# Residual loads and stores of two image pairs at a time in a 3x3 convolution with residual add

## Chip, cores, metric

One core of a Trainium2 chip. The metric is the device time in microseconds (us) of one execution; lower is better. Beside the timed figure, every run lists the span of its core, which is the time from the program's first to its last instruction; the difference between the two is called "the part outside the span" below.

## The reference

A 3x3 convolution, padding 1, plus a residual, all float32: x and residual are 16 x 64 x 64 x 64 (16.8 MB each), the weight is 64 x 64 x 3 x 3, the output is 16.8 MB.

```python
for b in range(batch):
    for co in range(c_out):
        for ci in range(c_in):
            for kh in range(k):
                for kw in range(k):
                    output[b, co] += weight[co, ci, kh, kw] * x_pad[b, ci, kh:kh+h, kw:kw+w]
return (output + residual).astype(np.float32)
```

## The kernel before

Two images make a pair: 128 partitions (image and channel) of 4096 pixels, 2 MB. SyncE issues all large transfers but one (ScalarE loads half of the first x). ScalarE (ACT) casts x into bf16 with even and odd rows in different partitions, TensorE (PE) does 24 matmuls per image into one of two PSUM halves, VectorE (DVE) adds PSUM and residual in place in `ro`, and `ro` is stored. All 16 MB of residual stay in SBUF. Everything but the last stores stands in one critical section, with hand-written semaphores. At its end SyncE waits for all engines, then the last two stores are issued, and a second critical section on GpSimd waits for the earlier ones.

```python
    ro = [pool.tile([128, NPIX], FP32, name=f"ro{p}") for p in range(NPAIR)]   # 8 tiles of 2 MB
    # ...
    with tc.tile_critical(no_gpsimd_drain=True):
        for p in range(NPAIR):
            if p >= NXR:                                     # NXR = 3 buffers of x
                nc.sync.wait_ge(s_half, 2 * (p - NXR) + 3)
            # ... (the weight is loaded after the first half of x)
                load_x(p)
            load_ro(p)                                       # a semaphore of its own
        for p in range(NEARLY):                              # NEARLY = 6
            nc.sync.wait_ge(s_add, 2 * p + 3)
            store(p).then_inc(s_out, 16)
        # ... (identity, zeros, casts of x and of the weight)
        for n in range(B):
            p, im = divmod(n, 2)
            # ...
            if im == 0:
                nc.vector.wait_ge(s_r[p], 16)
            # ... two adds per image
        # ... (TensorE)
    for p in range(NEARLY, NPAIR):                           # two stores of 2 MB
        store(p)
    with tc.tile_critical(sync_engine=mybir.EngineType.Pool, no_gpsimd_drain=True):
        nc.gpsimd.wait_ge(s_out, 16 * NEARLY)
```

## Time and profile before

| | before |
|---|---|
| time, median of 3 | 122.9 us (122.8 to 123.06) |
| span of the profiled run | 121.2 us |
| bytes moved | 33.70 MB read, 16.78 MB written |
| DMA rate, slices 4 to 38 | 427 or 433 GB/s in all but three |
| PE ends / DVE ends / last store lands | 99.5 / 104.1 / 120.2 us |

How to read it: the DMA engines are full from about 3 us to 119 us, so the time is bytes over rate plus a start and an end. The lines that carry this are in the prediction.

### The profile page before, as it was taken

To read this page: it belongs to the slowest core of one execution; us is meant where nothing else is said; L and a number is where in the kernel's file an instruction comes from. 1 tells how busy PE (TensorE), PEld (TensorE's weight loads), DVE (VectorE), ACT (ScalarE), POOL (GpSimd) and SP (SyncE) were. 2 spreads that over 40 slices of the span, in tenths; PEclk is the share of its full clock that TensorE was granted. 3 is DMA by queue.
4 is the path that set the end of the run, shared out by engine and by line. 5 is a ranking of instruction groups with operands and counts; after the bars stand their busy time and mean duration, and the time that the engine had idled before them with its cause. 6 is when DMAs were issued, how large, how long until landed. Compare 5 with 4: busy or idle time off the path is not lost.

```text
span 121.2 us, 736 instructions
## 1 busy us (share of the span) xinstructions
PE 87.7 (72%) x389; PEld 10.7 (9%) x105; DVE 76.0 (63%) x40; ACT 63.1 (52%) x37; POOL 2.4 (2%) x16
## 2 busy tenths in 40 slices
PE   0033499999999999999999999999999980000000
PEld 0021001101010101010101010101010100000000
DVE  0005300889898898989889898898989889300000
ACT  4049969938966984993993994896000000000000
POOL 5200000000000000000000000000000000000000
PEclk9999999999999999999999999999999999755555
DMA  6999999999999999999999999999999999999993
GB/s 168 427 444 433 433 433 433 433 427 433 433 427 427 433 433 427 427 433 427 433 433 433 433 433 422 433 389 433 433 433 433 422 433 433 433 433 433 427 433 151
DMA packets 3744, 50.48 MB, mean 417 GB/s; under 512 B 416, under 2 KB 544, under 8 KB 544
## 3 DMA queue, kind: packets, MB, share of 16 engines
q1 hardware_dynamic: 3600, 49.43, 96.3%
q10 hardware_dynamic: 144, 1.05, 2.0%
HBM read 33.70 MB, written 16.78 MB: 417 GB/s over the span
## 4 chain that ended last, share of the span: by engine, by line
PE 71%; DVEq 2%; DVE 2%; issue 0%
PE ps L86 53%; PE ps L85 17%; DVEq L129 2%; DVE ro L201 2%
## 5 line engine op out<-in xcount | busy, mean ns | idle before, releaser
L201 DVE TENSOR_TENSOR ro<-ps,ro 64x2048 f32<-64x2048 f32 x32 | 73.2, 2289 | 17.7 <-PE ps L86 17.2
L86 PE MATMUL ps<-xp,wl 128*128 128x504 bf16 (+1 forms) x288 | 80.0, 388 | 0.2
L173 ACT CAST xp<-xr 64x2048 bf16<-64x2048 f32 x16 | 30.3, 1896 | 19.3 <-DMA xr<-in_x_dram 17.1
L85 PE MATMUL ps<-xp,wl 128*128 128x504 bf16 (+1 forms) x92 | 35.8, 389 | 3.4 <-PEq L222 3.4
L177 ACT CAST xp<-xr 64x2048 bf16<-64x2048 f32 x16 | 30.4, 1897 | 0.4
L85 PEld LDWEIGHTS ps<-xp,wl 128*128 128x128 bf16 x96 | 9.5, 99 | 79.1 <-issue 79.1
L189 DVE CAST wl<-ps 32x192 bf16<-32x192 f32 x8 | 2.8, 348 | 10.4 <-PE ps L214 10.3
L214 PE MATMUL ps<-ident,wraw 128*32 128x128 f32 x9 | 2.1, 412 | 8.1 <-DMA wraw<-in_weight_dram 8.1
L214 PEld LDWEIGHTS ps<-ident,wraw 128*32 128x32 f32 x9 | 1.2, 137 | 8.6 <-issue 8.1
L173 ACT ACT_TABLE_LOAD x1 | 1.3, 1283 | 1.1 <-SPq L129 1.1
L182 ACT CAST wl<-ps 32x192 bf16<-32x192 f32 x4 | 1.2, 306 | 0.0
L160 POOL MEMSET xp<- 64x64 bf16 x4 | 0.6, 147 | 0.2
L159 POOL MEMSET xp<- 64x64 bf16 x4 | 0.6, 145 | 0.2
L148 POOL TENSOR_SCALAR_AFFINE_SELECT ident<-ident 128x128 f32<-128x128 f32 x1 | 0.3, 295 | 0.2 <-POOL ident L146 0.2
L162 POOL MEMSET wl<- 64x192 bf16 x1 | 0.3, 253 | 0.1
L161 POOL MEMSET wl<- 64x192 bf16 x1 | 0.3, 252 | 0.1
L146 POOL MEMSET ident<- 128x128 f32 x1 | 0.2, 205 | 0.7 <-SPq L129 0.7
L257 POOL MEMSET const-uint8-127<- 128x1 uint8 x1 | 0.1, 113 | 0.0
L257 POOL MEMSET const-bfloat16-1.0<- 128x1 bf16 x1 | 0.1, 112 | 0.0
L257 POOL MEMSET const-float32-1.0<- 128x1 f32 x1 | 0.1, 109 | 0.0
L257 POOL MEMSET const-float32-0.0<- 128x1 f32 x1 | 0.1, 104 | 0.2 <-issue 0.2
## 6 DMA issues: line engine op xcount, KB each, us to landing
ro<-in_residual_dram SPq DMA_DIRECT2D x8, 2048.0 KB, 21.9
out_dram<-ro SPq DMA_DIRECT2D x8, 2048.0 KB, 28.2
xr<-in_x_dram SPq DMA_DIRECT2D x7, 2048.0 KB, 17.5
xr<-in_x_dram SPq DMA_DIRECT2D x1, 1024.0 KB, 7.0
xr<-in_x_dram ACTq DMA_DIRECT2D x1, 1024.0 KB, 7.6
wraw<-in_weight_dram SPq DMA_DIRECT2D x1, 144.0 KB, 6.9
```

What stands on the lines that cost most here:

```text
L85: return e.matmul(out=out_, lhsT=lhsT, rhs=rhs, start=start, stop=stop, skip_group_check=True)
L86: return e.add_instruction(mybir.InstMatmult(name=nc.get_next_instruction_name(), engine=PE, ins=[e.lower_ap(rhs), e.lower_ap(lhsT)], outs ...
L129: with tc.tile_critical(no_gpsimd_drain=True):
L159: nc.gpsimd.memset(t[0:64, 0, :], 0.0).then_inc(s_id, 1)
L160: nc.gpsimd.memset(t[64:128, J, :], 0.0).then_inc(s_id, 1)
L173: i = nc.scalar.copy(out=t[64:128, 0:J, :], in_=x4[hp, :, 0, :])
L177: nc.scalar.copy(out=t[0:64, 1 : J + 1, :], in_=x4[hp, :, 1, :]).then_inc(s_pack, 1)
L182: i = nc.scalar.copy(**weight_block(h, *b))
L189: i = nc.vector.tensor_copy(**weight_block(h, *b))
L201: i = nc.vector.tensor_tensor(out=o4[hp, :, par, :], in0=psj[64 * par : 64 * par + 64, :, :], in1=o4[hp, :, par, :], op=ADD)
L214: i = nc.tensor.transpose(out=tp[0:32, t // 3, 128 * (t % 3) : 128 * (t % 3) + 128], in_=wraw3[:, :, t], identity=ident[:, :])
L257: nc = _bacc.Bacc("TRN2", target_bir_lowering=False, num_devices=1)
```

## The change

Its intent: fewer and larger transfers (4 MB), x loaded further ahead, one store and not two behind the critical section, and 13 semaphores where there were 20. The residual of pairs 2 and 3, 4 and 5, 6 and 7 comes in one transfer each, counted on two semaphores; DVE therefore waits five times and not eight. All stores are of two pairs.

```diff
-    NEARLY = 6
+    NSTORE = NPAIR // 2
+    RES = (slice(0, 1), slice(1, 2), slice(2, 4), slice(4, 6), slice(6, 8))
@@
-    ro = [pool.tile([128, NPIX], FP32, name=f"ro{p}") for p in range(NPAIR)]
+    ro = pool.tile([128, NPAIR, NPIX], FP32)
@@
-    s_r = [sem(f"s_r{p}") for p in range(NPAIR)]
+    s_r = [sem(f"s_r{i}") for i in range(2)]
...  (s_wt is dropped, its counts go on s_id)
@@
-    def load_ro(p):
-        nc.sync.dma_start(out=ro[p][:, :], in_=res_bc[128 * p : 128 * p + 128, :]).then_inc(s_r[p], 16)
-
-    def store(p):
-        return nc.sync.dma_start(out=out_bc[128 * p : 128 * p + 128, :], in_=ro[p][:, :])
+    def load_ro(i):
+        if i >= 2:
+            nc.sync.wait_ge(s_r[i % 2], 16 * (i // 2))
+        nc.sync.dma_start(out=ro[:, RES[i], :], in_=res_bc[:, RES[i], :]).then_inc(s_r[i % 2], 16)
+
+    def store(k):
+        pairs = slice(2 * k, 2 * k + 2)
+        return nc.sync.dma_start(out=out_bc[:, pairs, :], in_=ro[:, pairs, :])
@@
-            load_ro(p)
-        for p in range(NEARLY):
-            nc.sync.wait_ge(s_add, 2 * p + 3)
-            store(p).then_inc(s_out, 16)
+            if p in (0, 1, 3, 5, 7):
+                load_ro((p + 1) // 2)
+        for k in range(NSTORE - 1):
+            nc.sync.wait_ge(s_add, 4 * k + 5)
+            store(k).then_inc(s_out, 16)
@@
-            if im == 0:
-                nc.vector.wait_ge(s_r[p], 16)
+            if im == 0 and p in first:
+                i = first.index(p)
+                nc.vector.wait_ge(s_r[i % 2], 16 * (i // 2 + 1))
@@
-    for p in range(NEARLY, NPAIR):
-        store(p)
+    store(NSTORE - 1)
     with tc.tile_critical(sync_engine=mybir.EngineType.Pool, no_gpsimd_drain=True):
-        nc.gpsimd.wait_ge(s_out, 16 * NEARLY)
+        nc.gpsimd.wait_ge(s_out, 16 * (NSTORE - 1))
```

More of the change, by code (lines that the diff above doesn't have):

```diff
@@ L37 @@
     NXP = 4
-    NEARLY = 6
-    res_bc = residual.rearrange("b c h w -> (b c) (h w)")
-    out_bc = out.rearrange("b c h w -> (b c) (h w)")
+    NZERO = 4 + 2 * NXP
+    NSTORE = NPAIR // 2
+    RES = (slice(0, 1), slice(1, 2), slice(2, 4), slice(4, 6), slice(6, 8))
+    res_bc = residual.rearrange("(p b) c h w -> (b c) p (h w)", b=2)
+    out_bc = out.rearrange("(p b) c h w -> (b c) p (h w)", b=2)
     x_bc = x.rearrange("b c h w -> (b c) (h w)")
@@ L59 @@
     s_x = [sem(f"s_x{i}") for i in range(NXR)]
-    s_r = [sem(f"s_r{p}") for p in range(NPAIR)]
+    s_r = [sem(f"s_r{i}") for i in range(2)]
     s_out = sem("s_out")
     s_id = sem("s_id")
-    s_wt = sem("s_wt")
     s_half = sem("s_half")
@@ L178 @@
             if n == 0:
-                nc.scalar.wait_ge(s_wt, 1)
+                nc.scalar.wait_ge(s_id, NZERO + 1)
                 for b in blocks[4:]:
@@ L182 @@
                         i = nc.scalar.copy(**weight_block(h, *b))
-                i.then_inc(s_wt, 1)
-        nc.vector.wait_ge(s_wt, 1)
+                i.then_inc(s_id, 1)
+        nc.vector.wait_ge(s_id, NZERO + 1)
         for k, b in enumerate(blocks[:4]):
@@ L191 @@
                     i.then_inc(s_bank, 2)
-        i.then_inc(s_wt, 1)
+        i.then_inc(s_id, 1)
+        first = [pairs.start for pairs in RES]
         for n in range(B):
@@ L195 @@
             hp = slice(64 * im, 64 * im + 64)
-            o4 = ro[p].rearrange("q (j two w) -> q j two w", two=2, w=W)
+            o4 = ro[:, p, :].rearrange("q (j two w) -> q j two w", two=2, w=W)
             psj = ps[n % 2].rearrange("q c j w -> q (c j) w")
-            if im == 0:
-                nc.vector.wait_ge(s_r[p], 16)
+            if im == 0 and p in first:
+                i = first.index(p)
+                nc.vector.wait_ge(s_r[i % 2], 16 * (i // 2 + 1))
             for par in range(2):
@@ L207 @@
                 i.then_inc(s_add if par == 0 or n == B - 1 else s_bank, 1)
-        nc.tensor.wait_ge(s_id, 4 + 2 * NXP)
+        nc.tensor.wait_ge(s_id, NZERO)
         nc.tensor.wait_ge(s_w, 16)
@@ L216 @@
             )
-        i.then_inc(s_wt, 1)
-        nc.tensor.wait_ge(s_wt, 3)
+        i.then_inc(s_id, 1)
+        nc.tensor.wait_ge(s_id, NZERO + 3)
         with nc.Fori(0, B // NXP, 1, engines=[PE]):
```

## The prediction

> **What bounds the kernel now.** I read the page's slices first, then the chain, then the DMA queue's own waits, then a table by stage, then the times at which single transfers landed.
>
> ```profile
> DVE  0005300889898898989889898898989889300000
> DMA  6999999999999999999999999999999999999993
> GB/s 168 427 444 433 433 433 433 433 427 433 433 427 427 433 433 427 427 433 427 433 433 433 433 433 422 433 389 433 433 433 433 422 433 433 433 433 433 427 433 151
> DMA packets 3744, 50.48 MB, mean 417 GB/s; under 512 B 416, under 2 KB 544, under 8 KB 544
> HBM read 33.70 MB, written 16.78 MB: 417 GB/s over the span
> PE 71%; DVEq 2%; DVE 2%; issue 0%
> ```
>
> The DMA row is full in 38 of 40 slices at one rate, whether it reads (first two thirds) or writes (last third). The chain says "PE 71%", but its last pieces end at about 104 us: PE finishes at 99.5, DVE at 104.1, and the span is 121.2. The last 17 us are stores, so the chain names an engine that is merely nearly as long, and the bound is the DMA. The stage table says the same (columns: window, length, busy time by engine, clock, DMA share, GB/s):
>
> ```profile
> 3.00:4.00 1.00, 0.00 (x0) 0.00 (x0) 0.00 (x0) 0.00 (x0) 0.78 (x5) 1.00 1.00 418
> 40.00:80.00 40.00, 39.90 (x185) 4.48 (x46) 35.16 (x16) 31.40 (x17) 0.00 (x0) 1.00 1.01 427
> 80.00:100.00 20.00, 19.43 (x90) 2.14 (x22) 17.56 (x9) 3.87 (x3) 0.00 (x0) 1.00 1.00 430
> 100.00:118.00 18.00, 0.00 (x0) 0.00 (x0) 4.09 (x2) 0.00 (x0) 0.00 (x0) 0.62 1.01 431
> 119.00:120.00 1.00, 0.00 (x0) 0.00 (x0) 0.00 (x0) 0.00 (x0) 0.00 (x0) 0.50 0.20 82
> ```
>
> So the time is a sum: about 1.1 us to the first packet, then 50.48 MB at about 429 GB/s = 117.7 us (with the thin second microsecond, data end at about 119.3), then about 1.9 us for the last write's receipt (last landing near 120.2) and the closing barriers (to 121.2). The timed 122.9 is 1.7 above the span. The change leaves the bytes alone. It can only alter the rate, the start, the end, or whether the queue ever runs dry.
>
> **What the Trainium skill says.** (1) "DMA: Bandwidth & Descriptors", section "Where 436 GB/s comes from", gives a fabric ceiling of 435 GB/s; the trace holds 427 to 433, so it is at that ceiling and there is nothing to gain in rate. (2) The same page, "Rules for kernel authors", asks for at least 1 MiB per DMA: transfers are 2 MB already, and in the trace the 2 MB ones follow each other at the ceiling, so 4 MB should buy nothing. (3) The same page, "Queues, rings and completion order": each DMA engine takes the descriptors of a ring in order. The trace agrees (landings below come in issue order, about 4.86 us per 2 MB), and I use it to move landings around. (4) The same page, "Latency and other measured facts", reports slow copies where the rows are a large power of two apart, 2 MiB among them. A 4 MB transfer here visits two 16 KB rows 2 MiB apart per partition; the kernel before has no such transfer, so its trace says nothing of it. It is my main doubt.
>
> **The change part by part.**
>
> Descriptors: every row stays one run of 16 KB (64 x 64 floats), so the number of data packets is the same. What goes is completion packets: the page has 416 packets under 512 B, which is 26 transfers x 16. Afterwards there are 18 on the SP queue and 1 on the ACT queue, 19 x 16 = 304, so 112 fewer, 7 per DMA engine. Those last some 8 ns each in the trace's packet records against 611 ns for a 16 KB one: 7 x 8 ns = 0.06 us. That is on the path, and all that surely is.
>
> SP's issue time: an issue costs it 0.33 to 0.53 us, and with 8 MB or more queued behind it this lies beside other work. Half the issues saved is worth 0.
>
> Order of loads. Before: x0 r0 x1 r1 x2 r2 x3 r3 ... After: x0 r0 x1 r1 x2 x3 r2+r3 x4 x5 r4+r5 x6 x7 r6+r7. By position in the queue the double loads end exactly where r3, r5 and r7 ended, x3, x5 and x7 land one place (4.86 us) earlier, the other x stay, and r2, r4 and r6 are late by one place. The trace gives the landings:
>
> ```profile
> 20.08 0.43 SPq L76 DMA_DIRECT2D ro<-in_residual_dram  x1
> 39.60 0.43 SPq L76 DMA_DIRECT2D ro<-in_residual_dram  x1
> 59.09 0.43 SPq L76 DMA_DIRECT2D ro<-in_residual_dram  x1
> ...
> 42.46 4.61 DVE L201 TENSOR_TENSOR ro<-ps,ro 64x2048 f32<-64x2048 f32 x2 [0.58 <-PE ps L86]
> ```
>
> With 22.0, 22.0 and 22.2 us from issue to landing, r3 lands at 42.1, r5 at 61.6, r7 at 81.3. (r5 minus r3 is 19.5 us for 8 MB, hence 4.86 per 2 MB.) When does DVE need them? The add of image 15 starts at 99.52 and images are 5.19 us apart, so image 4 (first of pair 2) starts at 42.46, image 8 at 63.2, image 12 at 84.0. The double loads are in time by 0.4, 1.6 and 2.7 us. If the first were late, the 0.58 us that DVE waits in each image for PE is a second cushion before PE feels it. So these loads are just in time, by design.
>
> Does the queue run dry with the new waits? x3 is issued when image 2's first cast is done, 19.7 us as before; r1 and x2 are then outstanding, until 27.5. x4 at 29.5: behind it x3 (to 32.3) and r2+r3 (to 42.1). x5 at about 37: r2+r3 and x4 to 47. x6 at 49: x5 and r4+r5 to 61.6. x7 at about 56.5 (before 58.7): r4+r5 and x6 to 66. Never under 7 us of backlog. The new waits on the residual semaphores are for transfers that landed long before.
>
> Stores. The first needs the first half of image 4's add (44.8) and follows the last load at once at about 57; the second needs image 8's (65.5), the third image 12's (86.3). Load data end at about 81, then each store takes 9.7 us: to 91, 100, 110. All are queued before their turn.
>
> The end. Here the kernel before shows how much slack there is:
>
> ```profile
> SPq L71 <- ACT xp L173: 51.4, 5, 15.7
> SPq L79 <- DVE ro L201: 24.9, 4, 10.0
> SPq L129 <- DVEq L129: 17.4, 1, 17.4
> SPq L268 <- DMA out_dram<-ro: 14.8, 2, 10.0
> ...
> 104.42 0.96 SPq L79 DMA_DIRECT2D out_dram<-ro  x2
> DMA to landing us min/median/max: 10.9/13.2/15.4
> ```
>
> SP stands 17.4 us at the end of the critical section, issues the last two stores at 104.42 (just after DVE), and they land at 115.3 and 120.2. The sixth store, issued at 86.27 and 24.2 us on its way, lands at 110.5, so 104.4 leaves the new store about 5 us of queue ahead of it (estimate; about 4 once some 1.1 us from issue to first packet are taken off). Afterwards one 4 MB store is issued at the same moment and moves the same bytes: end at 120.2 again. One final DMA wait instead of two saves nothing, since the second alone ends last.
>
> Semaphores: 20 to 13 changes no instruction count on POOL, DVE or ACT; the closing clear is a single range instruction of 0.2 us before as after (the instruction lists show it). Fewer waits on DVE, ACT and PE are off the path. At most 0.1 us.
>
> Sum: 122.9 - 0.06 - (0 to 0.1) = **122.8 us**.
>
> **The rivals.**
>
> 1. Residual double loads come late, DVE stalls PE, and PE's end moves. For: the first margin is 0.4 us only. Against: a slip up to 4 us is absorbed by the queue in front of the last store. A slip of 2 us gives 122.8; 6 us would give about 125. Under 2%.
>
> 2. The 2 MiB stride slows the transfers. For: the skill's figure. Against: that is for 128 rows each at that pitch, here two rows; the DMA engines move a 16 KB packet in 611 ns for read and write alike, so they and not HBM are the limit. If 29.4 MB (three loads, four stores) ran 5% slower, +3.4 us: 126.3, slower by 2.8%. I give it 3%.
>
> 3. Larger transfers remove bubbles and gain 1 us or more. Against: the DMA share is already 1.00 between 3 and 119 us; the one dip (389 GB/s at about 80 us, some 0.3 us) sits where loads turn to stores, and that turn stays. Faster by 2% needs 2.5 us, and start, dip and end together hold hardly more than 3.
>
> **Range and chances.** Three runs lay within 122.8 to 123.06; with 0.3% for chip and run, and a tail for rivals 1 and 2, 122.2 to 123.5 should hold 8 in 10. Faster by over 2%: 2%; within: 95%; slower: 3%.
>
> **What would show it right or wrong.** Right: DMA row at 9 in 38 slices and 427 to 433 GB/s; packets under 512 B down from 416 to 304; the first double residual landing at about 42 us with DVE's add of image 4 not waiting for it by more than half a microsecond; x3 landing near 32; PE's end within 1 us of 99.5; the last store issued at 104 to 105 and landing at about 120. Wrong: a lower GB/s in the slices of double loads or stores (rival 2), a DVE wait on the residual load followed by gaps of PE (rival 1), a DMA slice under 9 between loads and stores or before the last store, or DMA ending early, which would mean that bubbles did cost.

## The result, and the profile after

The changed kernel took 123.56 us (median of 6, 123.44 to 123.79) against 122.9 us (median of 6): ratio 1.0051, interval 1.0037 to 1.0066. It is 0.5% slower, within 2% as forecast, but just above the stated range (122.2 to 123.5), and in the opposite direction to the forecast saving. Ratios are the mean time of one kernel's runs over that of the other's of the same rounds, so not quite the ratio of the medians quoted. (In the table of experiments below, the ratios come out when the first run of each kernel, the profiled one, is left out; the means there include it.)

The page of the changed kernel, slices and packets:

```profile
span 121.7 us, 730 instructions
DMA  6999999999999999999999999999999999999991
GB/s 170 425 450 431 431 431 436 431 436 436 431 431 431 431 431 431 431 431 431 431 431 431 431 431 431 393 425 431 431 425 431 431 431 436 431 431 436 431 431 59
DMA packets 3632, 50.48 MB, mean 415 GB/s; under 512 B 304, under 2 KB 432, under 8 KB 432
```

As predicted: the DMA row is as full as before at the same rate, also in the slices of 4 MB loads and stores; one dip to 393 remains where loads turn to stores; the small packets fell from 416 to 304. The last slice moves less (59 GB/s against 151): a slice is a fortieth of the span, so with a longer span the last one begins later, after more of the data. The bulk of the data is not late, yet the span is longer. In the packet records the last completions of the 16 DMA engines come at 119.5 us on average before and 119.4 after; only the very last data packet ends 0.2 us later, at 120.07 against 119.87.

The tightest load is the first double residual load. It was issued at 20.16, and another view gives 22.0 us until it landed, so it landed at 42.2. DVE's timeline of the changed kernel shows who waited for it:

```profile
42.25 4.61 DVE L208 TENSOR_TENSOR ro<-ps,ro 64x2048 f32<-64x2048 f32 x2 [0.74 <-DMA ro<-in_residual_dram]
47.27 4.61 DVE L208 TENSOR_TENSOR ro<-ps,ro 64x2048 f32<-64x2048 f32 x2 [0.41 <-PE ps L90]
...
99.22 4.61 DVE L208 TENSOR_TENSOR ro<-ps,ro 64x2048 f32<-64x2048 f32 x2 [0.58 <-PE ps L90]
```

DVE waited 0.16 us longer than its usual 0.58. The next image's add started on time and the later ones about 0.08 us late (52.54, where 5.19 us an image from 36.89 would give 52.46); the last image's add starts at 99.22, where it stood at 99.52 before. The loads are just in time, and harmless.

What did change is in SyncE's own waits. The changed kernel:

```profile
SPq L72 <- ACT xp L178: 50.8, 5, 16.2
SPq L83 <- DVE ro L208: 27.5, 2, 20.3
SPq L133 <- DVEq L133: 17.4, 1, 17.4
SPq L274 <- POOLq L247: 16.2, 1, 16.2
```

Columns: who waits, for whom, us in total, times, longest. Before, the last of these lines read "DMA out_dram<-ro: 14.8, 2": the program ended on a transfer. Now it ends on GpSimd's sequencer (L247 is the second critical section). The records of single instructions in the trace show why. Time in us, length in ns, engine, and in my words what it does; other engines, and GpSimd's last steps after, are left out:

```
before                                              after
115.372  28 Sync   wait (first late store landed)   120.433 383 Sync   wait (the only late store landed)
115.380  43 GpSimd wait (the same)                  120.441  43 GpSimd wait (the same)
115.466  33 GpSimd branch                           120.527  33 GpSimd branch
115.615  17 GpSimd signals SyncE                    120.676  17 GpSimd signals SyncE
115.710  13 GpSimd no-op, to 115.85 drain           120.771  13 GpSimd no-op
120.230  28 Sync   wait (second late store landed)  120.856   7 Sync   drain (waits for GpSimd)
120.297   7 Sync   drain                            120.916   7 Sync   drain
120.357   7 Sync   drain
120.390  17 GpSimd closing barrier                  120.998  17 GpSimd closing barrier
```

From the last landing to the closing barrier it is 0.16 us before and 0.565 us after. GpSimd's closing steps wait for the first store behind the critical section. With two stores there, they ran while the second was under way. With one, they follow the last landing. The rest of the difference between these two profiles is 0.2 us of later landing (120.43 against 120.23), as late as the last data packet. That is the scatter of single runs: the mean span of the kernel before over the 34 runs timed beside the experiments is 121.35, so its profile, at 121.2, is a low one, and the six runs of the changed kernel have a mean span of 121.47, so its profile, at 121.7, is a high one. In the other sixteen profiles the last data packet ends between 119.73 and 120.30, with all stores of 2 MB (120.03 in e12, 120.16 in e5) as with larger ones.

The other part is seen only by subtraction (spans are listed to 0.1 us, so one run's figure is good to 0.05). Timed minus span is 2.06 to 2.15 us (mean 2.11) in each of the six runs of the changed kernel, and 1.77 to 1.88 (mean 1.82) in each of the 34 of the kernel before. So 0.28 us were lost where no view looks.

### The profile page after: what moved, and what is told of

It reads as the page before. It is cut to its first block, busy times and chain, and to the rows that moved or that the text cites. A ratio compares the mean times of both kernels' runs of the same rounds, so it can differ in the third digit from the quotient of the medians.

```text
span 121.7 us, 730 instructions
## 1 busy us (share of the span) xinstructions
PE 87.5 (72%) x393; PEld 10.6 (9%) x105; DVE 76.0 (62%) x40; ACT 63.1 (52%) x37; POOL 2.4 (2%) x16
## 4 chain that ended last, share of the span: by engine, by line
PE 70%; DVEq 2%; DVE 2%; issue 0%
PE ps L90 52%; PE ps L89 18%; DVEq L133 2%; DVE ro L208 2%
```

## Experiments

Theory A: GpSimd's closing steps behind the only late store cost 0.4 us. Theory B: 4 MB transfers, with their 2 MiB stride, move slower or end less even. Theory C: something of the program costs 0.28 us outside the span; at first the number of semaphores was suspected, then the length of an engine's program (DVE has 62 instructions before and 59 after, SyncE 46 and 39). All sixteen runs are in the table, with means over each kernel's runs; "before" is of the same rounds on the same chip (four jobs, four chips; the kernel before had 1.82 or 1.83 us outside the span on each). "DVE" is the number of instructions of DVE's program as built, waits included.

| run | DVE | time | span | outside | before: time, span | ratio (interval) |
|---|---|---|---|---|---|---|
| e1_split_last | 59 | 123.27 | 121.17 | 2.10 | 123.13, 121.30 | 1.0009 (0.9994 to 1.0024) |
| e2_one_behind | 62 | 123.46 | 121.65 | 1.81 | same | 1.0027 (1.0010 to 1.0044) |
| e3_tail_merged | 62 | 123.46 | 121.62 | 1.84 | same | 1.0020 (1.0002 to 1.0037) |
| e4_sems20 | 59 | 123.69 | 121.60 | 2.09 | same | 1.0042 (1.0027 to 1.0057) |
| e5_after_loads_before_stores | 59 | 123.45 | 121.36 | 2.09 | 123.21, 121.38 | 1.0019 (1.0001 to 1.0036) |
| e6_after_order_2mb_loads | 62 | 123.59 | 121.78 | 1.81 | same | 1.0031 (1.0013 to 1.0049) |
| e7_dve_waits | 62 | 123.02 | 121.20 | 1.82 | same | 0.9983 (0.9967 to 1.0000) |
| e8_sp_waits | 59 | 123.40 | 121.32 | 2.08 | same | 1.0012 (0.9995 to 1.0029) |
| e9_dve_60 | 60 | 123.41 | 121.17 | 2.24 | 123.21, 121.39 | 1.0010 (0.9993 to 1.0027) |
| e10_dve_61 | 61 | 123.46 | 121.25 | 2.21 | same | 1.0014 (0.9997 to 1.0031) |
| e11_dve_65 | 65 | 123.27 | 121.22 | 2.04 | same | 0.9998 (0.9981 to 1.0015) |
| e12_before_dve_59 | 59 | 123.33 | 121.25 | 2.09 | same | 1.0006 (0.9989 to 1.0022) |
| e13_dve_63 | 63 | 123.01 | 121.10 | 1.91 | 123.18, 121.36 | 0.9982 (0.9956 to 1.0007) |
| e14_dve_64 | 64 | 123.09 | 121.13 | 1.95 | same | 0.9988 (0.9955 to 1.0020) |
| e15_dve_66 | 66 | 123.50 | 121.30 | 2.20 | same | 1.0022 (0.9987 to 1.0056) |
| e16_dve_70 | 70 | 123.26 | 121.43 | 1.83 | same | 1.0002 (0.9977 to 1.0027) |

### One store or two behind the critical section

**e1_split_last**, the changed kernel with the last store cut in two:

```diff
-    store(NSTORE - 1)
+    for p in (NPAIR - 2, NPAIR - 1):
+        nc.sync.dma_start(out=out_bc[:, p, :], in_=ro[:, p, :])
```

> The changed kernel, its last 4 MB store alone cut into two of 2 MB, both behind the critical section. Theory A (GpSimd's closing steps wait for the only store behind the critical section, so they run after the last landing and no longer beside it): the step from the last landing to the closing barrier falls from 0.56 us back to about 0.16 us, the time falls by 0.4 us or more, to 122.9 to 123.2. Theory B (4 MB transfers at a 2 MiB stride move slower or leave the DMA engines uneven): the three other large stores and the three large loads stay, so the time stays at 123.4 to 123.6. Theory C (fewer semaphores or instructions shift something outside the profiled span): stays near 123.5.

Measured 123.27, just above the 122.9 to 123.2 that theory A was given, but 0.42 us under e4 (the changed kernel with idle semaphores, same job). SyncE again ends on a transfer:

```profile
SPq L133 <- DVEq L133: 17.4, 1, 17.4
SPq L275 <- DMA out_dram<-ro: 15.2, 2, 10.4
```

In the trace's records the landing is at 120.403 and the barrier at 120.563: 0.16 us again. Theory A holds; the three other large stores are still there, so B is not the 0.4 us.

**e2_one_behind**, the kernel before with one store of 2 MB behind, the opposite edit:

```diff
-    NEARLY = 6
+    NEARLY = 7
```

> The kernel before, with seven 2 MB stores inside the critical section and one behind it instead of six and two; all else as it was, all transfers of 2 MB. Theory A: GpSimd's closing steps fall behind the last landing, 0.4 us between landing and barrier is added, ratio 1.003 to 1.005 against before. Theory B and C: no double transfer, no change of semaphores, so 1.000 within 0.001.

Measured 1.0027, a little under the expected 1.003 to 1.005; span 0.35 us longer, outside unchanged. The wait on GpSimd appears in a kernel without any 4 MB transfer, and the landing-to-barrier step is 0.565 us (120.231 to 120.796):

```profile
SPq L79 <- DVE ro L201: 35.1, 5, 10.0
SPq L268 <- POOLq L241: 15.6, 1, 15.6
SPq L129 <- DVEq L129: 7.0, 1, 7.0
```

**e3_tail_merged**, the kernel before with its last two stores as one of 4 MB:

```diff
-    for p in range(NEARLY, NPAIR):
-        store(p)
+    nc.sync.dma_start(out=out_pp[:, NPAIR - 2 :, :], in_=last[:, :, :])
```

(`last` holds pairs 6 and 7, `out_pp` is the output seen by pairs.)

> The kernel before, with the last two 2 MB stores merged into one of 4 MB behind the critical section, all else of 2 MB as before. Theory A: +0.4 us as in the run with one 2 MB store behind. Theory B in its narrow form (the last transfer's 4 MB leave the DMA engines less even, so the last packet lands later): about 0.2 us more than the run with one 2 MB store behind, 123.4 to 123.6 in all, with the last landing 0.2 us after the bulk of the data. Theory C: 122.9.

Measured 123.46, the same as e2 with 2 MB. A 4 MB last store costs what a 2 MB one costs in its place. Theory B in its narrow form has no support.

**e4_sems20**, the changed kernel with seven unused semaphores:

```diff
     s_add = sem("s_add")
+    spare = [sem(f"spare{i}") for i in range(7)]
```

> The changed kernel with seven unused semaphores allocated, 20 in all as before. Theory C (the number of semaphores matters): the closing range clear goes back from 0.157 to 0.200 us, and if the part of the time outside the span (2.1 us against 1.8 us) hangs on it, that falls as well, 123.2. Theories A and B: within 0.1 us of the changed kernel, 123.5 to 123.65.

Measured 123.69 and 2.09 outside. The closing range clear grew only from 0.157 to 0.184 us (expected 0.200). The number of semaphores is not the part outside the span.

### What costs 0.28 us outside the span

**e5_after_loads_before_stores**, loads and semaphores of the changed kernel, stores of before (short form):

```diff
-        for k in range(NSTORE - 1):
-            nc.sync.wait_ge(s_add, 4 * k + 5)
-            store(k).then_inc(s_out, 16)
+        for p in range(NEARLY):
+            nc.sync.wait_ge(s_add, 2 * p + 3)
+            store(p).then_inc(s_out, 16)
```

> Loads and semaphores of the changed kernel, stores of the kernel before (eight of 2 MB, two of them behind the critical section). The end is as before, so no 0.4 us from GpSimd's closing steps: inside the span about 121.2 on average, as in the run with only the last store split (121.17) and a little under the kernel before (121.30). The 0.28 us outside the span (timed minus span: 2.10 in the changed kernel and the two runs made from it, 1.82 in the kernel before and the two made from it): if 4 MB stores cause it, 1.82 here; if the loads, their semaphores or DVE's three waits fewer do, 2.10.

Outside 2.09, so the stores are not its cause. The span, 121.36, is that of the kernel before and not 121.2; half a prediction missed, within the scatter that remains below.

**e6_after_order_2mb_loads**, the changed kernel with each large residual load cut in two, a semaphore and a DVE wait per pair:

```diff
-        nc.sync.dma_start(out=ro[:, RES[i], :], in_=res_bc[:, RES[i], :]).then_inc(s_r[i % 2], 16)
+        for p in range(RES[i].start, RES[i].stop):
+            nc.sync.dma_start(out=ro[:, p, :], in_=res_bc[:, p, :]).then_inc(s_p[p], 16)
@@
-            if im == 0 and p in first:
-                i = first.index(p)
-                nc.vector.wait_ge(s_r[i % 2], 16 * (i // 2 + 1))
+            if im == 0:
+                nc.vector.wait_ge(s_p[p], 16)
```

> The changed kernel with each 4 MB residual load cut into two of 2 MB in the same order, each pair with a semaphore and a DVE wait of its own as before; stores as in the changed kernel. Inside the span 121.45 on average as in the changed kernel, since one store is behind the critical section. Outside the span: 1.82 if the 4 MB loads or DVE's fewer waits (59 instructions against 62) cause the 0.28 us, 2.10 if the stores or SyncE's shorter program do.

Outside 1.81. Either the 4 MB loads or the DVE waits do it. The span, 121.78, is 0.40 us over the kernel before of the same job, as one late store should make it; the expectation of 121.45 came from another job.

**e7_dve_waits**, e1 with DVE waiting at every pair again, on counts met long before:

```diff
-            if im == 0 and p in first:
-                i = first.index(p)
+            if im == 0:
+                i = next(k for k, pairs in enumerate(RES) if pairs.start <= p < pairs.stop)
                 nc.vector.wait_ge(s_r[i % 2], 16 * (i // 2 + 1))
```

> The changed kernel with its last store split, and DVE waiting at every pair for the residual semaphore, three waits more that are met long before, so that DVE's program has 62 instructions as in the kernel before. If the length of DVE's program causes the part outside the span: it falls from 2.10 to 1.82 and the time from 123.27 to 123.0, then faster than the kernel before by 0.1 us. If not: 2.10 and 123.27.

Outside 1.82, time 123.02: three waits that wait for nothing took 0.26 us off the part outside the span against e8 (next, same job, same transfers, 2.08), with 4 MB loads and stores in place. So it is DVE's waits and not the size of the transfers, and nothing is left for theory B to explain. This is also the fastest version settled with five timed runs: 0.9983 of the kernel before, 0.2 us, with an interval that just reaches 1.

**e8_sp_waits**, e1 with SyncE's program at its old length instead:

```diff
-            nc.sync.wait_ge(s_add, 4 * k + 5)
+            for v in range(4 * k + 1, 4 * k + 6):
+                nc.sync.wait_ge(s_add, v)
```

> The changed kernel with its last store split, and SyncE waiting for smaller values of the add semaphore ahead of each early store, six instructions more that change no issue time, so that its program has 46 instructions as in the kernel before. If the length of SyncE's program causes the part outside the span: 1.82 and 123.0. If not: 2.10 and 123.27.

Outside 2.08: six instructions more on SyncE (46, as before) do nothing.

**e12_before_dve_59**, the kernel before with its residual loads on two semaphores, DVE waiting five times; transfers as they were:

```diff
-    s_r = [sem(f"s_r{p}") for p in range(NPAIR)]
+    s_r = [sem(f"s_r{i}") for i in range(2)]
+    FIRST = (0, 1, 2, 2, 4, 4, 6, 6)
+    NEED = {0: (0, 16), 1: (1, 16), 2: (0, 48), 4: (1, 48), 6: (0, 80)}
...  (SyncE waits ahead of loads 2, 4 and 6 for the loads counted so far on that semaphore)
-            if im == 0:
-                nc.vector.wait_ge(s_r[p], 16)
+            if im == 0 and p in NEED:
+                nc.vector.wait_ge(s_r[NEED[p][0]], NEED[p][1])
```

> The kernel before, its eight residual loads of 2 MB counted on two semaphores so that DVE waits five times and not eight, 59 instructions; transfers, their order and both stores behind the critical section as before. If DVE's program length is the cause: outside the span 2.09, and the kernel before becomes 0.27 us slower, ratio 1.002. If the cause was something else in the changed kernel: 1.82 and 1.000. Inside the span 121.3 to 121.4 either way.

Outside 2.09, as forecast, in the kernel before. The total rose by 0.12 us only and not by the forecast 0.27, since its span came out 0.14 us shorter, though the transfers are those of before; the ratio of the times, 1.0006, is not clear of 1.

### How it depends on DVE's length

e9, e10, e13, e14, e15 and e16 are e1 with 1, 2, 4, 5, 7 and 11 such waits more; e11 has six more in a row ahead of DVE's first copy. The form of the edit, here for e10 and for e15 (on e7):

```diff
-            if im == 0 and p in first:
-                i = first.index(p)
+            if im == 0 and (p in first or p in (3, 5)):
+                i = next(k for k, pairs in enumerate(RES) if pairs.start <= p < pairs.stop)
```
```diff
-            if im == 0:
+            for _ in range((im == 0) + (im == 1 and p < 4)):
```

And for e11:

```diff
+        for v in range(1, 13):
+            nc.vector.wait_ge(s_id, v)
```

(two waits share an instruction, so twelve make six).

> The changed kernel with its last store split, and one of the three DVE waits put back (at pair 3): DVE's program has 60 instructions. So far 59 gave 2.08 to 2.10 us outside the span (six kernels) and 62 gave 1.82 (five kernels). If the part falls in proportion to the length: 2.00. If it is a step with a threshold: 2.09 or 1.82, nothing between.

> The same with two DVE waits put back (pairs 3 and 5): 61 instructions. In proportion: 1.91. A step: 2.09 or 1.82.

> The changed kernel with its last store split, with six DVE waits more in a row ahead of its first copy, met as soon as the first wait is: 65 instructions, at another place than in the runs before. If it is the length that counts and not what stands where: 1.82 or, in proportion, about 1.55. If the place counts: 2.09. Inside the span no change, 121.2.

> The changed kernel with its last store split and DVE's program at 63 instructions, by waits already met. Outside the span so far: 59 2.09, 60 2.24, 61 2.21, 62 1.82, 65 2.04. If it repeats every four instructions: about 2.09 as 59. If 62 was the one good length: above 2.0 here and in the next three. If it only gets shorter beyond 61: 1.8 or less, against the 65.

> The same with 64 instructions. Every four: about 2.24 as 60.

> The same with 66 instructions. Every four: 1.82 as 62, and the time about 0.2 us under the kernel before. Every eight or not periodic: something else, above 2.0.

> The same with 70 instructions. Every four or every eight: 1.82 as 62. Not periodic: anything.

Measured, by length: 59 2.09, 60 2.24, 61 2.21, 62 1.82, 63 1.91, 64 1.95 (three runs at 1.80, 1.97 and 2.09), 65 2.04, 66 2.20, 70 1.83 us. Neither proportion nor one threshold, and no period of four (66 is 2.20). The range is 0.42 us. The figures are steady where they can be compared: taken from the profiled runs alone, whose span the records give to the ns, the six kernels with 59 have 2.06 to 2.07 and the five with 62 have 1.82 to 1.83.

62 and 70 look equal, as if the part repeated every eight instructions. The records of e16's profile show that they are not: its delay is there, but inside the span. Time in us, length in ns:

```
e7, 62 instructions                             e16, 70 instructions
120.706  21 Vector waits for GpSimd             120.685  21 Vector waits for GpSimd
120.816  10 Vector drain, signals GpSimd        121.195 134 Vector drain, signals GpSimd
121.042  34 GpSimd drain                        121.021  34 GpSimd drain
121.120  17 GpSimd last closing barrier         121.363  17 GpSimd last closing barrier
```

Between two of its closing instructions DVE takes 0.51 us in e16 and 0.11 us in e7 and in all the other profiles, and the last barrier comes 0.26 us later for it. From the closing barrier of the records further above to the end of the timed figure it is 2.82 us in e16, 2.56 in e7, and 2.79 to 2.80 in e1, e5 and e8 with 59. So in this one profile the lost time lies on DVE itself, behind the last landing. That it is the same delay at the other lengths, fallen behind the last record, is likely but not shown.

What holds DVE there stays open, and one rival is untested: the supply of its instructions. The packet records, which no view shows, have 8 KB packets of a kind called "instruction". All profiles have some before the program starts; the four with 64, 65, 66 and 70 instructions have one more after the last record, 1.84, 1.79, 1.67 and 0.32 us behind it, and the fourteen with 59 to 63 have none there. This alone does not explain 59 to 61, which lose time without such a packet.

Nor is the number of waits told apart from their place. e11 was to do that, with 1.82 or about 1.55 expected if the length counts and 2.09 if the place does: 2.04 is nearer to the latter, but since the other lengths scatter from 1.82 to 2.24 it decides nothing. No two kernels have the same length with the waits at different places.

## Why the prediction was wrong

**Right.** The bound, and that the transfers would not notice: 425 to 436 GB/s from the fourth slice to the last but one, apart from the one dip; small packets 304; the first double load at 42.2 (forecast 42) and DVE waiting 0.16 us over its usual 0.58; x3 issued at 19.8 and on its way for 12.7 us, so at 32.5 (forecast 32); the last image's add at 99.2, so PE's end within 0.3 us of the forecast 99.5; last store issued at 104.1 and landed at 120.4. Rivals 1 and 2 did not occur. Rival 3 did not either. The bulk term of the sum, more than 117 us, was right.

**Wrong, first step.** "One final DMA wait instead of two saves nothing, since the second alone ends last." True of SyncE, and silent on GpSimd, whose closing steps also wait for the first late store. They cost 0.40 us in the records (0.565 - 0.16), 0.35 us of span when added to the kernel before (e2), 0.43 us of span when taken away (e4 against e1). Term forecast: 0. The instruction records of the kernel before show it beforehand: GpSimd waits for the first late transfer at 115.38. No view that I read showed it.

**Wrong, second step.** "Fewer waits on DVE, ACT and PE are off the path." Off the path inside the span, yes. But I added the 1.7 us above the span as a constant, and with DVE's three waits less it rose by 0.28 us in the changed kernel and by 0.26 us where nothing else differs much (e7 against e8, e12 against the kernel before). That DVE's waits move it is shown; how they do it is open.

**The sum.** Inside the span, ten of the eleven kernels with the changed loads and two late stores (e1, e5, e7 to e11, e13 to e15) lie between 0.26 and 0.02 us under the kernel before of their job, 0.15 under it on average; the eleventh, e16, lies 0.07 over it, and its profile has DVE's 0.26 us inside the span. Some 0.05 us of the saving stands in the records: from the closing barrier to the last record it is 0.782 us before and 0.728 in the changed kernel, with a range clear of 0.200 and 0.157 us for 20 and 13 semaphores. The forecast saving of 0.06 to 0.16 us is of that size, but e12 has it as well (0.14) without any large transfer, and the scatter from kernel to kernel is as large, so for the rest it isn't shown where it comes from. 0.4 + 0.28 - 0.15 = 0.53; e4 over the kernel before of its job: 0.56 us. In the first job it was 0.63 us, on other runs of the kernel before.

**Slips in the working**, none of which moved the forecast. The span of 121.2 belongs to a run timed at 123.0, so 1.8 us and not 1.7 lie above it. The data do not end at 119.3: by the packet records the 16 DMA engines end between 119.29 and 119.87, the last about 0.35 us before its data count as landed. An issue costs SyncE up to 0.58 us (the second late store), and a completion packet 9 ns. r2, landed with r3, is two places late and not one. Only DVE has fewer instructions (62 to 59); ACT and PE have as many as before. And 611 ns a packet both ways (429 GB/s for 16 DMA engines) makes the DMA engines the likely limit, but no run separates them from the rest of the way to HBM.

## What to carry to other kernels

Where the data end on time and the span does not, read the waits of the queue that ends last, and ask which steps at the close could run beside the last transfer: two late stores gave them cover, one did not. A timed figure less the span is a quantity to watch on its own; here a change to one engine's wait instructions that cost nothing inside the span moved it by 0.28 us. Read the closing records with it: a small difference can also mean that the same delay fell inside the span (e16). At 0.5% compare means of many runs of both kernels on one chip, since a single profile may be 0.2 us off its own kernel's mean.

## What the Trainium skill lacked or had wrong

- "Runtime: NRT & Kernel Launch", section "The ~15µs preamble/postamble breakdown", lets the total of the stages around a kernel depend on engine count and DMA setup, and has nothing on the length of an engine's program. Here the timed figure exceeds the span by 1.82 to 2.24 us, by the number of DVE instructions (62: 1.82, 60: 2.24), while SyncE's changed nothing (2.08 to 2.11 at 39, 40, 43 and 46 of them, with 59 of DVE).
- No page has that a framework's closing section on GpSimd costs 0.4 us (0.565 against 0.16 us from landing to barrier) when it has to wait for the last transfer, and nothing when it waits for the one before.
- "DMA: Bandwidth & Descriptors", section "Latency and other measured facts", on rows a large power of two apart: two rows 2 MiB apart per partition cost nothing here (431 GB/s in slices of such loads and of such stores). The page speaks of copies between HBM tensors with 128 rows at that pitch, so it isn't wrong, but it doesn't say from how many rows on it matters.
- "DMA: Bandwidth & Descriptors", section "Where 436 GB/s comes from", says that for transfers between HBM and SBUF the HBM side, about 358 GB/s a core, binds. For a program on one core it doesn't: most slices hold 425 to 436 GB/s, reads and writes alike, near the page's fabric ceiling of 435. The page's own table one section up, measured with the pair's other core idle, has 425 and agrees.
